# GpSimd writes the low half of a split weight tile in four pieces instead of one operation

## The chip, the core and the metric

The kernel runs on one core of a Trainium2 chip. Its time is the device time of one execution in microseconds (us), given as the median of several runs. The core's engines run their own instruction queues side by side and wait for one another by semaphores: TensorE (PE in the profile, with PEld for its weight loads), VectorE (DVE), ScalarE (ACT), GpSimd (POOL) and SyncE (SP, which issues most transfers).

## The reference, cut to what matters

One inference step of a two-layer model on 128 context tokens and 512 latent tokens (640 in all) of width 1024. Layer 0 mixes by a gated linear attention beside a latent attention, layer 1 by differential attention; each layer ends in a gated MLP.

```
for l in range(2):
    h  = modulate(rmsnorm(x, norm_gain[l, 0]), shift, scale)
    # layer 0: gated linear attention and latent attention, then one output projection
    # layer 1: q, k, v = split(h @ w_in_odd); rotary positions on q and k of the latent tokens
    #          per head: p = softmax(q1 k1) - lam * softmax(q2 k2); o = p @ v
    x  = x + gate * mixer(h)
    h  = modulate(rmsnorm(x, norm_gain[l, 1]), ...)
    u  = conv3(h @ w_up);  a, g = split(u)
    x  = x + gate * ((silu(a) * g) @ w_down)
y = rmsnorm(x, final_gain)
```

All of it is float32. The kernel gets close to that with three matmuls of a shorter type: every operand is written as a high half and a low half, and hi·hi + hi·lo + lo·hi is summed.

## The kernel before, in words

Activations lie with the 1024 features on the partitions (8 tiles of 128) and the 640 tokens along the free axis; `A` and `B` each hold such an array as a pair (high half, low half). Weights come from memory as tiles `wraw` of 128 partitions x 1024 numbers, seen as [128, 8, 128] (8 blocks `k` of 128 columns) or [128, 4, 256]. `Weights.split` (lines 161 to 166) makes the pair: ScalarE copies `wraw` into `whi` (line 163), and the engine that `eng` names subtracts `whi` from `wraw` into `wlo` (line 165). That engine is VectorE in most places and GpSimd in 33: in 5 tiles of the first projection (`ada0`, shape [128, 2, 512]), in 3 tiles of the MLP's `up` of each layer (line 959), and, from `W.eng = G` (line 1138) on, in 22 tiles in the stretch of layer 1's differential attention (19 of its projections, 3 of the output projection that follows).

In that attention the heads come in pairs. While the heads of one pair are worked on, `diff_units` makes the queries, keys and values of the next pair as filling between the steps: `unit_qk` (line 1062) multiplies a weight tile with `B` in two halves of 320 tokens (`proj_half`, matmuls `qko` at line 211), and rotates the result with `rope` (lines 475 to 481). In `rope` VectorE shuffles (`rsh`, line 478) and multiplies (line 479), GpSimd multiplies `f` by `ropeC` (line 480), and VectorE adds the two (line 481); `split` (lines 172 and 173) then makes the pairs `kd` and `qd`. A step of the attention itself (`Attn`) is: scores (PE, `sc`, line 826), minimum (DVE, `mn`, line 851) and exponential (ACT, `p`, line 852); the two maps are combined into `p` (ACT line 1098, then DVE line 1099, which reads two arrays of 128 x 768 from SBUF); PE transposes `p` (`ptp`, line 869), ACT and DVE write the pair `pt` from PSUM (lines 177 and 178), and PE multiplies by the values (`pv`, line 883).

```
S.copy(out=hi, in_=raw)
lo = self.tile("lo", shape, FP32R)
(eng or self.eng).tensor_tensor(out=lo, in0=raw, in1=hi.bitcast(FP32), op=ALU.subtract)
```

The order of the instructions on each engine is set when the program is built: a scheduler goes through the operations in the order of the code, with a timing model of its own, and places each on its engine's queue. Waits are set by regions: an instruction waits for those that wrote what it reads.

Of the kernel before, what the change touches and what calls it, by code (L numbers as in the profile page):

```python
# [7 lines left out]
FP32 = mybir.dt.float32  # L8
# [6 lines left out]
ALU = mybir.AluOpType  # L15
# [41 lines left out]
def build(tc, a):  # L57
    nc = tc.nc
    V, S, G, PE = nc.vector, nc.scalar, nc.gpsimd, nc.tensor
# [77 lines left out]
    class Weights:  # L137
# [23 lines left out]
        def split(self, raw, shape, eng=None):  # L161
            hi = self.tile("hi", shape, FP32R)
            S.copy(out=hi, in_=raw)  # L163
            lo = self.tile("lo", shape, FP32R)
            (eng or self.eng).tensor_tensor(out=lo, in0=raw, in1=hi.bitcast(FP32), op=ALU.subtract)  # L165
            return hi, lo

        def close(self):
# [129 lines left out]
    def apply_norm(tp, x, bc, hl, l, n, half, k0=0, k1=KT):  # L298
        c0, c1 = CH[half]
        for k in range(k0, k1):  # L300
            t = tp.tile([128, CUT], FP32, tag="nm_t", name="nm_t", bufs=3)[:, 0:c1 - c0]
            hi, lo = [z[:, k, c0:c1] for z in hl]
            for s0, s1, c in seg(c0, c1):
                r = slice(s0 - c0, s1 - c0)
                u, sh = t[:, r], mods[l][:, 3 * n * KT + k, c:c + 1]
                V.scalar_tensor_tensor(out=u, in0=x[:, k, s0:s1], scalar=gs[l][:, n, k, c:c + 1], in1=bc[:, r],  # L306
                                       op0=ALU.mult, op1=ALU.mult)
                S.activation(out=u if k % 2 else hi[:, r], in_=u, func=ACTF.Identity, bias=sh)
                if k % 2 == 0:
                    last = V.scalar_tensor_tensor(out=lo[:, r], in0=u, scalar=sh, in1=hi[:, r].bitcast(FP32),  # L310
                                                  op0=ALU.add, op1=ALU.subtract)
            if k % 2:
                split(t, hi, lo, G)
        return last
# [83 lines left out]
    V.memset(csil, 0.0)  # L398
    tables(S.activation(out=csil[:, :, 0:2], in_=sm["cT"], func=ACTF.Silu))
    split(csil[:, :, 0:2], csr[:, :, 0:2], csr[:, :, 2:4])  # L400

    awp, awes = pool("aw", side="left")
# [110 lines left out]
    def logsig(c):  # L513
        e = ab[:, c].rearrange("p (d n) -> p d n", d=2)
        V.scalar_tensor_tensor(out=e, in0=zmm(c), scalar=0.0, in1=e, op0=ALU.min, op1=ALU.subtract)
        split(ab[:, c].rearrange("p (g t) -> p g t", g=4), *[z[:, :, c * 128:(c + 1) * 128] for z in la])
# [35 lines left out]
    for q in range(4):  # L552
        w = W(a["wva"][q], [128, 2, 512])
        for kk in range(2):
            k = 2 * q + kk
# [799 lines left out]
```

## Time and profile before

| what | value |
|---|---|
| median of 3 runs | 1824.09 us (1821.87 to 1824.63) |
| the profiled execution | 1819.55 us, its span 1817.8 us |
| PE busy | 1744.3 us, 96% of the span |
| DVE busy | 1272.0 us, 70% |
| ACT busy | 758.9 us, 42% |
| POOL busy | 294.7 us, 16% |

The span is the part of the execution between the first and the last instruction; the rest of the profiled execution's time lies around it. The durations below come from this one execution. Times in rows are microseconds from the start of the span unless a column says ns.

### The profile page before, as it was taken

Reading aid. Unit: us, or ns where it says so; the run is one execution under the profiler, and the core shown is the slowest. Engines: PE = TensorE matmul, PEld = TensorE weight load, DVE = VectorE, ACT = ScalarE, POOL = GpSimd, SP = SyncE. Lnnn points to the kernel's source line nnn. Section 1 sums busy time; section 2 is a strip of 40 time slices with the busy share of each in tenths; the row PEclk is TensorE's granted clock in tenths of the full one; section 3 lists DMA queues with packets and bytes.
Section 4 is the critical chain, followed back from the end, with each engine's and each line's share of the span. In section 5 each row is a group of like instructions: output and inputs, shape, how many; then the busy total and the mean of one; then the engine's idle time right before and its main releaser. Section 6 shows DMA issues by size and latency. Waiting matters only on the chain. (4 is left out here: it accounts for less than half of the span.)

```text
span 1817.8 us, 29362 instructions
## 1 busy us (share of the span) xinstructions
PE 1744.3 (96%) x11716; PEld 1634.6 (90%) x11716; DVE 1272.0 (70%) x2438; ACT 758.9 (42%) x1344; POOL 294.7 (16%) x246
## 2 busy tenths in 40 slices
PE   7999989999999999999999999999999999999996
PEld 1898776889999999999988989897989999999996
DVE  5964877778699999946588787876475554545556
ACT  6444434544532232323356665665373232322232
POOL 3201021000310100100133232321031010101004
PEclk9999999999999999999999989998999999999998
DMA  9650001044256555412231021111122222222121
GB/s 372 198 166 9 28 3 72 4 175 139 93 174 189 171 176 184 156 59 88 65 123 61 31 58 42 63 49 70 59 70 81 82 70 79 73 73 79 59 82 58
DMA packets 57336, 176.58 MB, mean 97 GB/s; under 512 B 6064, under 2 KB 11568, under 8 KB 56816
## 3 DMA queue, kind: packets, MB, share of 16 engines
q1 hardware_dynamic: 53408, 160.59, 27.4%
q0 software_dynamic: 3792, 14.13, 2.2%
q8 instruction: 92, 1.51, 0.3%
q14 instruction: 44, 0.36, 0.1%
HBM read 166.59 MB, written 7.77 MB: 96 GB/s over the span
## 5 line engine op out<-in xcount | busy, mean ns | idle before, releaser
L202 PE MATMUL up<-B,whi 128*128 128x320 f32 x2560 | 479.6, 309 | 0.0
L163 ACT CAST whi<-wraw 128x1024 fp32r<-128x1024 f32 (+2 forms) x208 | 208.3, 1002 | 506.7 <-PE up L202 231.3
L202 PEld LDWEIGHTS up<-B,whi 128*128 128x128 f32 x2560 | 401.6, 188 | 0.0
L165 DVE TENSOR_TENSOR wlo<-wraw,whi 128x1024 fp32r<-128x1024 f32 (+2 forms) x175 | 204.2, 1167 | 226.3 <-ACT whi L163 226.0
L202 PE MATMUL up<-B,wlo 128*128 128x320 f32 x1280 | 291.8, 309 | 0.0
L202 PE MATMUL po<-A,whi 128*128 128x320 f32 x1312 | 246.3, 310 | 0.7 <-DVE u L967 0.5
L202 PEld LDWEIGHTS up<-B,wlo 128*128 128x128 f32 x1280 | 213.8, 188 | 0.0
L363 DVE CUSTOM_DVE_ANT_0 junk<-araw,cbc 128x1024 bf16<-128x1024 f32 x160 | 203.5, 1272 | 12.2 <-DMA araw<-in_wada0b 9.4
L202 PEld LDWEIGHTS po<-A,whi 128*128 128x128 f32 x1312 | 205.7, 188 | 1.5 <-issue 0.7
L173 POOL TENSOR_TENSOR A<-u,A 128x640 fp32r<-128x640 f32 x44 | 76.1, 1730 | 758.2 <-ACT A L172 733.2
L202 PE MATMUL po<-A,wlo 128*128 128x320 f32 x656 | 149.8, 310 | 0.5 <-DVE wlo L165 0.5
L211 PE MATMUL qko<-B,whi 128*128 128x320 f32 x512 | 121.6, 322 | 2.4 <-ACT B L172 1.5
L340 PE MATMUL pot<-A,whi 128*128 128x320 f32 x512 | 113.9, 312 | 0.0
L202 PEld LDWEIGHTS po<-A,wlo 128*128 128x128 f32 x656 | 109.5, 188 | 0.8 <-DVE wlo L165 0.8
L165 POOL TENSOR_TENSOR wlo<-wraw,whi 128x1024 fp32r<-128x1024 f32 x33 | 79.1, 2400 | 146.9 <-ACT whi L163 146.5
L965 DVE SCALAR_TENSOR_TENSOR u<-up,small,u 128x127 f32<-128x127 f32 (+1 forms) x176 | 95.5, 543 | 10.4 <-ACT u L963 9.5
L967 DVE SCALAR_TENSOR_TENSOR u<-up,small,u 128x127 f32<-128x127 f32 (+1 forms) x176 | 96.3, 548 | 4.5
L852 ACT ACTIVATE p<-sc,mn 128x768 f32<-128x768 f32 (+1 forms) x100 | 79.2, 797 | 39.8 <-DVE mn L851 39.3
L211 PEld LDWEIGHTS qko<-B,whi 128*128 128x128 f32 x512 | 89.0, 196 | 5.2 <-ACT B L172 1.8
L851 DVE TENSOR_REDUCE mn<-sc 128x1 f32<-128x768 f32 (+1 forms) x100 | 79.3, 816 | 16.1 <-PE sc L826 15.3
L340 PEld LDWEIGHTS pot<-A,whi 128*128 128x128 f32 x512 | 85.7, 188 | 1.1 <-issue 0.4
L202 PE MATMUL pe<-B,whi 128*128 128x320 f32 x416 | 81.2, 317 | 4.3 <-DVE nm_t L306 3.6
(294 smaller groups left out, 3056.0 us busy)
## 6 DMA issues: line engine op xcount, KB each, us to landing
wraw<-in_wup SPq DMA_DIRECT2D x88, 512.0 KB, 3.6
araw<-in_wada SPq DMA_DIRECT2D x48, 512.0 KB, 3.4
wraw<-in_wdn SPq DMA_DIRECT2D x40, 512.0 KB, 3.6
araw<-in_wada0b SPq DMA_DIRECT2D x32, 512.0 KB, 4.3
wraw<-in_wie SPq DMA_DIRECT2D x13, 512.0 KB, 4.4
aw<-in_wada0a SPq DMA_DIRECT2D x8, 512.0 KB, 8.8
wraw<-in_wada0a SPq DMA_DIRECT2D x8, 512.0 KB, 8.0
wraw<-in_woe SPq DMA_DIRECT2D x8, 512.0 KB, 4.3
```

The costliest lines, as they stand in the source:

```text
L163: S.copy(out=hi, in_=raw)
L165: (eng or self.eng).tensor_tensor(out=lo, in0=raw, in1=hi.bitcast(FP32), op=ALU.subtract)
L173: return (lo_eng or V).tensor_tensor(out=lo, in0=src, in1=hi.bitcast(FP32), op=ALU.subtract)
L202: PE.matmul(out=o, lhsT=w[wi][:, k], rhs=hl[ri][:, k, c0:c1], start=k == 0 and n == 0, stop=k == nk - 1 and n == 2)
L211: PE.matmul(out=o, lhsT=w[wi][:, k], rhs=hl[ri][:, k, c0:c1], start=k == 0 and n == 0, stop=k == nk - 1 and n == 2)
L340: PE.matmul(out=o, lhsT=ws[j + m][wi][:, k], rhs=hl[ri][:, k, c0:c1], start=k == 0 and n == 0, stop=k == nk - 1 and n == 2)
L363: V.tensor_tensor_reduce(out=junk, in0=raw, in1=self.cbc[:, j], op0=ALU.mult, op1=ALU.add, scale=1.0, scalar=0.0, accum_out=mods[l][:, t0 ...
L851: V.tensor_reduce(out=mn[:, m:m + 1], in_=ss[m][:, 0:nk], op=ALU.min, axis=AX.X)
L852: self.exp = S.activation(out=p[:, m, 0:nk], in_=ss[m][:, 0:nk], func=ACTF.Exp, scale=-1.0, bias=mn[:, m:m + 1], accum_out=li[:, m:m + 1])
L965: V.scalar_tensor_tensor(out=u[:, s0 + 1:s1], in0=r[:, s0:s1 - 1], scalar=cw[:, 0:1], in1=u[:, s0 + 1:s1], op0=ALU.mult, op1=ALU.add)
L967: last = V.scalar_tensor_tensor(out=u[:, s0:s1 - 1], in0=r[:, s0 + 1:s1], scalar=cw[:, 2:3], in1=u[:, s0:s1 - 1], op0=ALU.mult, op1=ALU.add)
```

## The change

The subtraction on GpSimd is cut along the second axis of the tile when that axis divides by four: a tile [128, 8, 128] or [128, 4, 256] becomes four operations of 128 x 256. The tiles [128, 2, 512] of the first projection stay whole, and so does every tile that VectorE subtracts. 28 operations become 112.

```
             lo = self.tile("lo", shape, FP32R)
-            (eng or self.eng).tensor_tensor(out=lo, in0=raw, in1=hi.bitcast(FP32), op=ALU.subtract)
+            eng = eng or self.eng
+            n = shape[1]
+            step = n // 4 if eng is G and n % 4 == 0 else n
+            for k in range(0, n, step):
+                z = slice(k, k + step)
+                eng.tensor_tensor(out=lo[:, z], in0=raw[:, z], in1=hi[:, z].bitcast(FP32), op=ALU.subtract)
             return hi, lo
```

Five lines are added, so that line numbers after 165 are five higher in the changed kernel. Each `qko` group of matmuls, which waited once for its tile's `wlo`, now waits four times, ahead of the first matmul on each piece. SyncE's queue is the same. The scheduler's order moves a little on the other engines, all of it in the differential attention.

GpSimd's queue in the second pair of heads, before. The first row fetches cached keys; the second is the weight tile of a query projection (`wlo`); then the rotary multiplications of the second head's queries and of the next pair's keys.

```order
L1072 DMA fk<-in_dkc 128x256
L165 TENSOR_TENSOR wlo<-wraw,whi 128x1024
L480 TENSOR_TENSOR fq<-fq,ropeC 128x192
L165 TENSOR_TENSOR wlo<-wraw,whi 128x1024
L480 TENSOR_TENSOR fq<-fq,ropeC 128x320
L1078 DMA o_dk<-fk 128x128
L480 TENSOR_TENSOR fk<-fk,ropeC 128x192
L165 TENSOR_TENSOR wlo<-wraw,whi 128x1024
L480 TENSOR_TENSOR fk<-fk,ropeC 128x320
L1072 DMA fk<-in_dkc 128x256
```

The same stretch with the change:

```order
L1077 DMA fk<-in_dkc 128x256
L170 TENSOR_TENSOR wlo<-wraw,whi 128x256 x4
L485 TENSOR_TENSOR fq<-fq,ropeC 128x192
L170 TENSOR_TENSOR wlo<-wraw,whi 128x256 x4
L485 TENSOR_TENSOR fq<-fq,ropeC 128x320
L1083 DMA o_dk<-fk 128x128
L485 TENSOR_TENSOR fk<-fk,ropeC 128x192
L170 TENSOR_TENSOR wlo<-wraw,whi 128x256 x4
L485 TENSOR_TENSOR fk<-fk,ropeC 128x320
L485 TENSOR_TENSOR fq<-fq,ropeC 128x192
```

Each `wlo` is now four operations in the place of one, and the rotary multiplication behind it stays behind all four. At the end the fetch of cached keys and the multiplication of 192 query tokens have changed places.

VectorE's queue about 40 us later, in the step that makes the next pair's first keys and queries, before. `li` and `p` belong to the attention, `fk`, `fq`, `rsh`, `kd` and `qd` to the rotation, `vd`, `vf` and `pt` are written from PSUM:

```order
L481 TENSOR_TENSOR fk<-fk,rsh 128x320
L1097 TENSOR_SCALAR li<-li,scal 128x1
L1099 SCALAR_TENSOR_TENSOR p<-p,li 128x768
L173 TENSOR_TENSOR kd_10866<-fk,kd_10865 128x320
L478 STREAM_SHUFFLE rsh<-fq 128x192
L479 TENSOR_TENSOR rsh<-rsh,ropeS 128x192
L178 TENSOR_TENSOR vd_11067<-vo,vd_11066 128x256
L1050 COPY vf<-vo 128x256
L178 TENSOR_TENSOR pt_10974<-ptp,pt_10973 128x3x128
L481 TENSOR_TENSOR fq<-fq,rsh 128x192
L178 TENSOR_TENSOR pt_10974<-ptp,pt_10973 128x3x128
L173 TENSOR_TENSOR qd_11020<-fq,qd_11019 128x320
```

With the change:

```order
L1102 TENSOR_SCALAR li<-li,scal 128x1
L486 TENSOR_TENSOR fk<-fk,rsh 128x320
L1104 SCALAR_TENSOR_TENSOR p<-p,li 128x768
L483 STREAM_SHUFFLE rsh<-fq 128x192
L178 TENSOR_TENSOR kd_10899<-fk,kd_10898 128x320
L484 TENSOR_TENSOR rsh<-rsh,ropeS 128x192
L486 TENSOR_TENSOR fq<-fq,rsh 128x192
L183 TENSOR_TENSOR vd_11109<-vo,vd_11108 128x256
L1055 COPY vf<-vo 128x256
L178 TENSOR_TENSOR qd_11056<-fq,qd_11055 128x320
L183 TENSOR_TENSOR pt_11007<-ptp,pt_11006 128x3x128 x2
```

The two additions of the rotation (`fk<-fk,rsh`, `fq<-fq,rsh`) and the low halves behind them have moved by one to three places: the first addition to behind a small operation on `li`, the second, with `qd`, to ahead of the two writes of `pt`.

## Rows read from the trace of the kernel before

**Rows 1.** The page's head, and its part on the engines: busy time, share of the span, instructions.

```profile
span 1817.8 us, 29362 instructions
PE 1744.3 (96%) x11716; PEld 1634.6 (90%) x11716; DVE 1272.0 (70%) x2438; ACT 758.9 (42%) x1344; POOL 294.7 (16%) x246
```

**Rows 2.** The waits of PE over the whole span: who waited for whom, us in total, times, longest.

```profile
PE pv L883 <- DVE pt L178: 6.9, 6, 2.0
...
PE adaps L424 <- POOL wlo L165: 2.4, 2, 1.6
```

**Rows 3.** All instructions of line 165 (count, ns min/median/max, first and last start), and below it who waited for that line (us, times); of these the rows of PEld and those for tiles that VectorE subtracts are left out.

```profile
L165 POOL TENSOR_TENSOR wlo<-wraw,whi x33: 2344/2394/2822, 7.9 to 1361.5; 128x1024 fp32r<-128x1024 f32 x33
...
who waited for it (us, times):
...
  PE adaps L424: 2.4, 2
```

**Rows 4.** The timeline about 1053 us, by engine (DVE, then POOL, ACT, PE): start, duration, engine, line, output and inputs, count; in brackets the idle time before it and what ended it.

```profile
1053.02 3.48 DVE L1099 SCALAR_TENSOR_TENSOR p<-p,li 128x768 f32<-128x768 f32 x1 [0.93 <-ACT p L1098]
...
1056.70 1.00 DVE L178 TENSOR_TENSOR pt<-ptp,pt 128x384 fp32r<-128x384 f32 x2
...
1053.32 2.36 POOL L165 TENSOR_TENSOR wlo<-wraw,whi 128x1024 fp32r<-128x1024 f32 x1
...
1053.20 0.87 ACT L177 CAST pt<-ptp 128x384 fp32r<-128x384 f32 x2
...
1054.55 0.74 PE L261 MATMUL rb<-negs,racc 128*64 128x2 f32 x10
1057.30 1.62 PE L883 MATMUL pv<-pt,vd 128*128 128x256 f32 x9 [2.00 <-DVE pt L178]
```

**Rows 5.** The same place one pair of heads later: DVE, POOL, PE.

```profile
1138.47 3.48 DVE L1099 SCALAR_TENSOR_TENSOR p<-p,li 128x768 f32<-128x768 f32 x1 [0.93 <-ACT p L1098]
...
1138.76 2.36 POOL L165 TENSOR_TENSOR wlo<-wraw,whi 128x1024 fp32r<-128x1024 f32 x1
...
1142.74 1.71 PE L883 MATMUL pv<-pt,vd 128*128 128x256 f32 x9 [2.01 <-DVE pt L178]
```

**Rows 6.** And in the last pair.

```profile
1220.88 2.39 DVE L1099 SCALAR_TENSOR_TENSOR p<-p,li 128x768 f32<-128x768 f32 x1 [0.93 <-ACT p L1098]
...
1220.09 2.37 POOL L165 TENSOR_TENSOR wlo<-wraw,whi 128x1024 fp32r<-128x1024 f32 x1 [2.21 <-ACT whi L163]
...
1224.07 1.33 PE L883 MATMUL pv<-pt,vd 128*128 128x256 f32 x9 [0.92 <-DVE pt L178]
```

**Rows 7.** All instructions of line 1099: ns min/median/max.

```profile
L1099 DVE SCALAR_TENSOR_TENSOR p<-p,li x40: 334/1018/3481, 963.8 to 1263.8; 128x768 f32<-128x768 f32 x32, 128x128 f32<-128x128 f32 x8
```

**Rows 8.** Two places where GpSimd operations follow one another and VectorE wants two SBUF operands: the timeline about 984 us, POOL then DVE, and the final normalization, POOL then DVE.

```profile
984.06 2.37 POOL L165 TENSOR_TENSOR wlo<-wraw,whi 128x1024 fp32r<-128x1024 f32 x1 [4.49 <-ACT whi L163]
986.39 1.11 POOL L480 TENSOR_TENSOR fq<-fq,ropeC 128x320 f32<-128x320 f32 x1
...
985.68 1.09 DVE L479 TENSOR_TENSOR rsh<-rsh,ropeS 128x320 f32<-128x320 f32 x1
...
1798.46 8.42 POOL L1183 TENSOR_TENSOR x2t<-x2t,bcs 128x320 f32<-128x320 f32 x8 [5.55 <-DVE bcs L245]
...
1803.34 2.82 DVE L234 TENSOR_TENSOR racc<-racc,rsq 128x320 f32<-128x320 f32 x3
```

**Rows 9.** The timeline of POOL at two operations of 128 x 256 that follow one another directly.

```profile
294.19 0.73 POOL L173 TENSOR_TENSOR A<-oo,A 128x256 fp32r<-128x256 f32 x1 [0.88 <-ACT A L172]
294.88 0.73 POOL L709 TENSOR_TENSOR oo<-oo,ga 128x256 f32<-128x256 f32 x1
```

**Rows 10.** Stretches of the span: us, then PE, PEld, DVE, ACT, POOL busy (instructions), the granted PE clock as a share of full speed, DMA share, GB/s.

```profile
1058.10:1061.50 3.40, 3.40 (x17) 3.40 (x16) 3.23 (x13) 2.63 (x6) 0.00 (x0) 0.50 0.18 74
...
1068.40:1075.10 6.70, 6.70 (x25) 5.63 (x24) 6.36 (x13) 3.67 (x8) 0.80 (x1) 0.50 0.29 81
...
1143.50:1146.80 3.30, 3.30 (x15) 3.30 (x15) 3.14 (x13) 2.48 (x6) 0.00 (x0) 0.50 0.17 71
1225.40:1228.70 3.30, 3.30 (x15) 3.30 (x15) 3.09 (x15) 3.05 (x6) 0.00 (x0) 0.50 0.04 11
...
1147.00:1218.00 71.00, 70.48 (x532) 64.76 (x531) 55.48 (x128) 43.52 (x98) 20.26 (x16) 1.00 0.11 36
```

**Rows 11.** The timeline of PE at three other waits.

```profile
985.77 1.30 PE L826 MATMUL sc<-kd,qd 64*128 64x512 f32 x6 [0.86 <-ACT p L852]
...
1067.41 1.51 PE L826 MATMUL sc<-kd,qd 64*128 64x512 f32 x6 [0.52 <-ACT p L852]
...
1152.85 1.31 PE L826 MATMUL sc<-kd,qd 64*128 64x512 f32 x6 [0.52 <-ACT p L852]
```

**Rows 12.** The rotary multiplication behind a weight tile and the addition that reads it, at two places: POOL and DVE about 1089 us, then about 1235 us.

```profile
1089.55 0.89 POOL L480 TENSOR_TENSOR fk<-fk,ropeC 128x320 f32<-128x320 f32 x1
...
1090.95 0.49 DVE L481 TENSOR_TENSOR fk<-fk,rsh 128x320 f32<-128x320 f32 x1
...
1234.77 1.20 POOL L480 TENSOR_TENSOR fq<-fq,ropeC 128x320 f32<-128x320 f32 x1
...
1236.55 0.48 DVE L481 TENSOR_TENSOR fq<-fq,rsh 128x320 f32<-128x320 f32 x1
```

## The prediction

> **What bounds the kernel now.** I read the page's busy shares first: PE is busy 96% of the span, 1744.3 of 1817.8 us, and POOL 16% [rows 1]. What can be won beside faster matmuls is therefore PE's 73.5 idle us and the time it runs at a lower clock. The obvious reading of the change is that PE can start on a piece of `wlo` before the whole tile is there. The waits say this is worth nothing: PE waited for a `wlo` of GpSimd in two places only, both in the first projection (`adaps`, 2.4 us), and those tiles are not cut [rows 2, 3].
>
> So I looked at what a GpSimd subtraction does to others. PE's longest sum of waits that is not a start-up is `pv`, waiting for VectorE's `pt`: 6.9 us [rows 2]. The timeline shows why. At 1053.02 VectorE starts line 1099, an operation on two SBUF arrays whose median is 1.018 us [rows 7]; it takes 3.48 us. GpSimd's `wlo` runs from 1053.32 to 1055.68, and line 1099 ends at 1056.50, 0.82 us after it [rows 4]. VectorE's operation stands still while GpSimd's runs. ScalarE has done its half of `pt` by 1054.07, but VectorE's half is queued behind line 1099 and starts at 1056.70; PE idles 2.00 us. The same rows return one pair later (3.48 us, PE idle 2.01) [rows 5] and in the last pair (2.39 us, idle 0.92) [rows 6]. Behind each of the three idle times PE runs 3.3 to 3.4 us at a granted clock of 0.50, the lower of its two levels, 1.2 instead of 2.4 GHz [rows 10].
>
> **The change part by part.**
>
> *A shorter hold.* What matters is whether VectorE gets its operands at the end of a piece, when the next piece is already queued. Two rows say yes. At 986.39 the rotary multiplication follows `wlo` directly on GpSimd, yet line 479, held since 985.68, ends at 986.77, while the multiplication takes 1.11 us instead of the 0.89 of another of its size [rows 8, 12]. And where eight GpSimd operations of 320 columns run back to back (8.42 us, 1.05 each), three of VectorE's end in 2.82 us, 0.94 each, about one GpSimd operation apart: they take turns [rows 8]. A piece costs 0.73 us, by a GpSimd subtraction of the same 128 x 256 [rows 9].
>
> First place: the first piece ends at 1053.32 + 0.73 = 1054.05, line 1099 at 1054.05 + 0.82 = 1054.87 instead of 1056.50, 1.63 us earlier; `pt` follows, and PE's 2.00 becomes 0.37. Second place: 1138.76 + 0.73 + 0.83 = 1140.32 against 1141.95, again 1.63, leaving 0.38. Third: `wlo` starts first, at 1220.09. Its second piece starts near 1220.8, about when line 1099 does (1220.88), so this waits to about 1221.55 and ends at 1222.36 instead of 1223.27, 0.91 earlier; PE's 0.92 goes. Sum 1.63 + 1.63 + 0.91 = 4.2 us. Behind these places PE has work and was not waiting, so I count it whole. VectorE's and GpSimd's rows there keep their order.
>
> Here a rule of the Trainium skill can be weighed (SBUF — State Buffer, "Who interferes with whom"): a VectorE operation with two SBUF inputs and a GpSimd operation that reads SBUF exclude each other, and the one that issues first keeps the port for its whole instruction. The trace agrees with the exclusion but not with the order: line 1099 started 0.30 us before GpSimd and still lost 2.46 us [rows 4]. By the rule it would win its race in the first two places, nothing would be left to gain there, and the sum would be the 0.91 of the third. The trace shows the loss, so I go by the rows.
>
> *The clock.* At half speed 3.4, 3.3 and 3.3 us of work cost 1.7 + 1.65 + 1.65 = 5.0 us [rows 10]. Do they go with the idle times? After a wait of 0.52 us the clock stayed at 1.00 at 1152.85 (the stretch 1147 to 1218), and after another of 0.52 at 1067.41 it was 0.50 for 6.7 us [rows 10, 11]. So for the 0.37 that is left both ends have a row: 0 and 5.0 us. I take half, 2.5.
>
> *GpSimd's own time.* Four pieces of 0.73, started 0.69 apart, end 3 x 0.69 + 0.73 = 2.80 us after the first start, against 2.39: 0.41 us for each of 28 tiles, 11.5 us on an engine that is 84% idle. In the MLP (six tiles) nothing waits. In the attention the rotary multiplication is behind the pieces, and VectorE's addition reads it. The room is small: it ended at 1090.44 and was read at 1090.95 (0.51 us), and at 1235.97, read at 1236.55 (0.58) [rows 12]. 0.41 fits. If VectorE's line 479 (0.34 after a release) is let in between the pieces, 0.75 does not. The scheduler has put one to three other operations ahead of these additions in most such places, which gives part of it back. Ends: 0, and eight places at 0.75 - 0.51 = 0.24, about 2 us. I take 0.6.
>
> *Waits and order.* Three more waits a tile on PE cost nothing if the pieces are there. At the first place `qko` follows `pv`, which ended at 1058.92 [rows 4] and would end near 1057.3; the last piece, with line 1099 let in, is done at 1053.32 + 2.80 + 0.82 = 1056.94. The moved rows on VectorE put `qd` and an addition, about 0.35 + 0.47 us, ahead of `pt` in two steps where PE had no wait; I count 0, and the danger is in the rivals.
>
> Sum: -4.2 - 2.5 + 0.6 = -6.1 us. On the profiled execution 1819.55 becomes 1813.45. The median of the runs lies 4.54 us above that execution (1824.09), and I carry the difference over: **1818.0 us**. The measurement tells about 0.2% (3.6 us) from no change, so this is just outside.
>
> **The rivals.**
>
> 1. *The clock stays low and VectorE gives some back*: 4.2 gained, 0 from the clock, 2 lost: -2.2, 1821.9 us, not measurable. For it: the 0.50 after a wait of 0.52 us [rows 10, 11]. Against: in the next pair the same wait had none.
>
> 2. *No release between pieces*: GpSimd keeps the operands while its queue holds the next piece. Then line 1099 is held 0.41 us longer in three places: +1.2, 1825.3 us, the same. Against it both cases of rows 8; for it, that there other lines, not pieces of one tile, followed each other.
>
> 3. *Slower: the additions of the rotation wait for GpSimd.* Every VectorE operation let in between pieces delays the rest by 0.34 to 0.82 us. With two or three of them the multiplication ends 0.41 + 1.5, about 1.9 us later, against 0.5 to 0.6 us of room [rows 12], and VectorE, with `pt` and `mn` queued behind the addition, stands 1.3 us. At eight places that is 10.4 us, less the 4.2, and with two new stretches at half clock (3.4) +9.6: 1833.7 us. It decides from about 0.6 us a place on, where eight places outweigh the gain. Against: in rows 4 to 6 and 8 one such operation falls into each `wlo`, not three.
>
> 4. *More than forecast*: all 5.0 us of clock, the 6.7 us stretch at 1068.4 (3.35 us [rows 10]), which follows a wait in the same pair, and the 0.86 at 985.77, which falls into another `wlo` [rows 8, 11]: -4.2 - 5.0 - 3.35 - 0.86 = -13.4, 1810.7 us.
>
> **How the numbers follow.** The forecast 0.48 (1814.9 with all three stretches gone to 1819.9 with none), rival 1 0.17, rival 2 0.10, rival 3 0.12, rival 4 0.13. Faster by over 0.2% are the forecast and rival 4: 0.61. The same: 0.27. Slower: 0.12. The range reaches from rival 4 to rival 2, 1811 to 1826 us; outside it stay rival 3 and the far side of rival 4.
>
> **What would show it.** Right: GpSimd's line 170 with 117 instructions, pieces of about 0.73 us; line 1104 with a longest duration near 1.9 us instead of 3.48; the wait of `pv` for `pt` at about 3 us instead of 6.9; fewer stretches at 0.50 in the pairs; the `wlo` waits of PE still in `adaps` alone. Wrong: line 1104 still at 3 us or more (rival 2), waits of VectorE for GpSimd's line 485 (rival 3), or the waits gone but the same number of stretches at 0.50 (rival 1).

## The result, and the profile after

The changed kernel takes 1808.63 us (median of 4 runs, 1807.67 to 1814.41), the kernel before, run beside it, 1822.98 (4 runs, 1821.79 to 1824.63): ratio 0.9935, 95% interval 0.9911 to 0.996, faster by more than the 0.2% that can be told. The forecast was 1818.0 in a range of 1811 to 1826. The sign is right; the gain is larger than the forecast, and the median lies 2.4 us under the lower end, nearest to the fourth rival (1810.7). By the ratio, the 1824.09 us that the forecast started from become 1812.2, just inside the range. The profiled execution took 1809.02 us for a span of 1807.2.

The page's head and engines, as [rows 1]:

```profile
span 1807.2 us, 29445 instructions
PE 1740.0 (96%) x11716; PEld 1628.6 (90%) x11716; DVE 1263.0 (70%) x2438; ACT 759.9 (42%) x1344; POOL 312.0 (17%) x330
```

POOL has 84 instructions more (28 tiles times 3) and is busy 17.3 us longer. The span is cut here at the same two points of the program, the first and the last long wait of PE in the differential attention; first the kernel before, then the changed one (us, then PE, PEld, DVE, ACT, POOL busy, the granted clock of PE, DMA share, GB/s):

```profile
0.00:961.00 961.00, 920.91 (x6055) 842.14 (x6056) 739.92 (x1405) 387.95 (x679) 135.81 (x122) 0.99 0.38 125
961.00:1286.00 325.00, 310.79 (x2211) 282.85 (x2210) 246.70 (x561) 194.14 (x428) 90.61 (x75) 0.94 0.16 52
1286.00:1817.00 531.00, 512.61 (x3452) 509.66 (x3452) 285.36 (x473) 176.86 (x239) 68.33 (x49) 0.98 0.24 74
```

```profile
0.00:963.00 963.00, 923.36 (x6056) 842.48 (x6056) 741.02 (x1405) 388.23 (x679) 136.99 (x131) 0.99 0.38 125
963.00:1275.00 312.00, 303.72 (x2211) 276.38 (x2209) 236.10 (x561) 194.55 (x428) 105.38 (x141) 0.97 0.17 54
1275.00:1807.00 532.00, 512.90 (x3452) 509.69 (x3452) 285.86 (x473) 177.11 (x240) 69.60 (x58) 0.98 0.24 74
```

All of the gain is in the middle, 325 to 312 us for the same 2211 matmuls. PE's idle time there goes from 14.2 to 8.3 us (5.9 less) and its busy time from 310.8 to 303.7 (7.1 less), at a granted clock of 0.97 of full speed instead of 0.94. These are two single executions; how much of the clock goes with the change is taken up below. The first part is 2 us longer and the last 1.

The waits of PE, as [rows 2], the line of VectorE's operation, as [rows 7], and GpSimd's subtractions:

```profile
PE adaps L429 <- POOL wlo L170: 3.4, 2, 1.8
...
PE pv L888 <- DVE pt L183: 1.2, 3, 0.5
```

```profile
L1104 DVE SCALAR_TENSOR_TENSOR p<-p,li x40: 335/1018/1495, 965.4 to 1253.7; 128x768 f32<-128x768 f32 x32, 128x128 f32<-128x128 f32 x8
```

```profile
L170 POOL TENSOR_TENSOR wlo<-wraw,whi x117: 717/742/2466, 8.8 to 1353.3; 128x256 fp32r<-128x256 f32 x112, 128x1024 fp32r<-128x1024 f32 x5
```

PE's waits for a GpSimd tile are still in the first projection alone, so no wait shows that a piece ready early could have shortened. The wait of `pv` for `pt` is 1.2 us in all instead of 6.9. Line 1104 (1099 before) has 1.50 us at its longest, not 3.48. At the first place, as [rows 4] (timeline of DVE, POOL, PE):

```profile
1054.83 1.47 DVE L1104 SCALAR_TENSOR_TENSOR p<-p,li 128x768 f32<-128x768 f32 x1 [0.65 <-ACT p L1103]
...
1056.50 1.00 DVE L183 TENSOR_TENSOR pt<-ptp,pt 128x384 fp32r<-128x384 f32 x2
```

```profile
1054.83 0.56 POOL L1077 DMA_DIRECT2D fk<-in_dkc  x1
1055.41 3.68 POOL L170 TENSOR_TENSOR wlo<-wraw,whi 128x256 fp32r<-128x256 f32 x4
```

```profile
1056.89 0.74 PE L266 MATMUL rb<-negs,racc 128*64 128x2 f32 x10
1057.56 1.79 PE L888 MATMUL pv<-pt,vd 128*128 128x256 f32 x9
```

`pt` ends at 1057.50 and PE goes on at 1057.56 with no wait where it stood 2.00 us. But look at the durations: VectorE's 1.47 us end 0.89 us after the first piece began, and the four pieces take 3.68 us, not the 2.80 that the prediction worked out. VectorE, which began as the issue of the `fk` load began (1054.83), ended 0.91 us after this issue did; it did not wait for a piece, the first piece waited for it. The second place is the same (1.50 us). In the last pair, as [rows 6]:

```profile
1213.25 1.45 DVE L1104 SCALAR_TENSOR_TENSOR p<-p,li 128x768 f32<-128x768 f32 x1 [0.76 <-ACT p L1103]
```

```profile
1212.46 3.53 POOL L170 TENSOR_TENSOR wlo<-wraw,whi 128x256 fp32r<-128x256 f32 x4 [0.66 <-PE ptp L874]
```

Here the operation began behind a piece, was held to its end, and took 1.45 us, against 1.48 by the prediction.

### The profile page after: what moved, and what is told of

Same layout as the page of the kernel before. It is cut to its first block, busy times and chain, and to the rows that moved or that the text cites. A ratio compares the mean times of both kernels' runs of the same rounds, so it can differ in the third digit from the quotient of the medians.

```text
span 1807.2 us, 29445 instructions
## 1 busy us (share of the span) xinstructions
PE 1740.0 (96%) x11716; PEld 1628.6 (90%) x11716; DVE 1263.0 (70%) x2438; ACT 759.9 (42%) x1344; POOL 312.0 (17%) x330
## 3 DMA queue, kind: packets, MB, share of 16 engines
q8 instruction: 92, 1.51, 0.3%
## 5 line engine op out<-in xcount | busy, mean ns | idle before, releaser
L170 POOL TENSOR_TENSOR wlo<-wraw,whi 128x256 fp32r<-128x256 f32 (+1 forms) x117 | 97.8, 865 | 134.5 <-ACT whi L163 133.8
L856 DVE TENSOR_REDUCE mn<-sc 128x1 f32<-128x768 f32 (+1 forms) x100 | 79.2, 815 | 14.6 <-PE sc L831 14.2
```

What stands on the lines that cost most here:

```text
L170: eng.tensor_tensor(out=lo[:, z], in0=raw[:, z], in1=hi[:, z].bitcast(FP32), op=ALU.subtract)
L856: V.tensor_reduce(out=mn[:, m:m + 1], in_=ss[m][:, 0:nk], op=ALU.min, axis=AX.X)
```

## The experiments

Three theories were put against each other. A: the gain is the shorter hold of VectorE's line 1104. B: it is the new order of rows that the scheduler gives the attention when the program has other instructions. C: PE starts earlier on a piece. Later D to G, told in the expectations, ask why a piece holds VectorE less. Ratios are to the kernel before, run on the same chip beside the experiment; they compare all runs and are not the quotient of two medians. The line numbers of these kernels lie 0 to 4 above those of the changed one, so VectorE's line is 1104, 1106 or 1108.

### Which tiles carry the gain

First I took the tile that collides at the first two places for that of `q1`, the query weights of the second head of a pair.

```diff
-            step = n // 4 if eng is G and n % 4 == 0 else n
+            step = n // 4 if eng is G and self.q1 else n      # a1; a2: n % 4 == 0 and not self.q1
...
+                W.q1 = isq and h % 2 == 1
                 w = W(a["wqo" if isq else "wko"][h], [128, KT, 128])
+                W.q1 = False
```

> The tiles of the unit q1 (the query weights of the second head of a pair, four tiles) are subtracted in four pieces; the other 24 that the change splits go in one operation. The order of the rows is then that of the kernel before but for 4 rows of VectorE and 3 of PE. Theory A (the gain is VectorE's line 1104 held for one piece instead of a whole tile at the three places of the prediction, with the low clock behind them): nearly all of the change's gain is there, 1808 to 1815 us, ratio about 0.994; line 1104 at most near 1.9 us instead of 3.48; the idle times of 2.00, 2.01 and 0.92 us fall to 0.4 or less. Theory B (the gain is the moved order of the rows in the attention): no gain, 1819 to 1824 us, whatever line 1104 takes. Theory C (PE starts earlier on a piece of any tile): four of 28 tiles, a seventh of the gain, 1821 us.

> The counterpart: the 24 other tiles in four pieces, the tiles of q1 in one operation. The order of ScalarE's rows is that of the changed kernel, and so is that of PE and VectorE but for 3 and 4 rows. Theory A: line 1104 is held as before (3.4 to 3.5 us at its longest), PE's two idle times of about 2 us and the low clock behind them are back, 1819 to 1825 us, ratio 0.998 to 1.002. Theory B: all the gain, 1808 to 1811 us, ratio 0.9935. Theory C: six sevenths of the gain, 1811 us.

Splitting `q1` alone gives 1820.17 us, ratio 1.0001 (0.9987 to 1.0015); all the others but `q1` give 1811.88, 0.9964 (0.9947 to 0.9981). Taken as written this speaks for B. The timelines say that the premise was wrong: with `q1` alone split, the tile at the place is whole, and all is as before:

```profile
1055.15 2.36 POOL L170 TENSOR_TENSOR wlo<-wraw,whi 128x1024 fp32r<-128x1024 f32 x1
```

```profile
1054.51 3.81 DVE L1106 SCALAR_TENSOR_TENSOR p<-p,li 128x768 f32<-128x768 f32 x1 [0.59 <-ACT p L1105]
```

```profile
1059.12 1.92 PE L888 MATMUL pv<-pt,vd 128*128 128x256 f32 x9 [2.26 <-DVE pt L183]
```

It stands behind the loads of `vc` and `fk` on GpSimd, and is that of `q0` of the next pair. So the pair was run again with `q0` (three tiles are GpSimd's). These two kernels are a cleaner test than the first: with `q0` alone split every row of PE, VectorE and ScalarE stands in the order of before, with all but `q0` split in that of the changed kernel.

```diff
-            step = n // 4 if eng is G and n % 4 == 0 else n
+            step = n // 4 if eng is G and self.qz else n      # c1; c2: n % 4 == 0 and not self.qz
...
+                W.qz = isq and h % 2 == 0
                 w = W(a["wqo" if isq else "wko"][h], [128, KT, 128])
+                W.qz = False
```

> The tile that lies on VectorE's line 1104 at the first two places is that of q0, the query weights of the first head of the next pair (its rows on GpSimd stand behind the loads of vc and fk), not that of q1. Here only these three tiles are split, the rest of the kernel is that of before, with every row of PE, VectorE and ScalarE in the order of before. Theory A (shorter hold): line 1104's counterpart falls from 3.5 to about 2 us at its longest among the first two places, PE's 2.00 and 2.01 us fall to about 0.4 each, the 0.92 us in the last pair stays: 3.3 us, and up to 6.8 us with the low clock behind them; ratio 0.994 to 0.998. Theory B (moved order): ratio 1.000, within 0.0015, although the idle times shrink or not. Theory C (early start of PE on a piece): three of 28 tiles, ratio 0.999 or more.

> The counterpart: the changed kernel, but the three tiles of q0 in one operation each; every row of PE, VectorE and ScalarE stands in the order of the changed kernel. Theory A: line 1104 takes 3.4 to 3.5 us at two places again, PE's idle times there are back (1.5 to 2.0 us, twice), ratio to the kernel before 0.998 to 1.001. Theory B: all of the gain, ratio 0.993 to 0.995, and the two idle times do not matter. Theory C: nine tenths of the gain, 0.994.

Three tiles in four pieces: 1811.16 us, ratio 0.9956 (0.9937 to 0.9975). The other 25 in pieces and these three whole: 1823.88 us, 1.0005 (0.9987 to 1.0024). A holds; B falls (the changed order alone gains nothing that can be measured), and C falls too. The rows of the first, at the first place:

```profile
1057.76 1.18 DVE L1106 SCALAR_TENSOR_TENSOR p<-p,li 128x768 f32<-128x768 f32 x1 [0.94 <-ACT p L1105]
```

```profile
1057.48 0.56 POOL L1079 DMA_DIRECT2D fk<-in_dkc  x1
1058.06 3.66 POOL L170 TENSOR_TENSOR wlo<-wraw,whi 128x256 fp32r<-128x256 f32 x4
```

```profile
1059.96 1.65 PE L888 MATMUL pv<-pt,vd 128*128 128x256 f32 x9
```

The rows of the second, with the order of the changed kernel:

```profile
1055.33 3.65 DVE L1106 SCALAR_TENSOR_TENSOR p<-p,li 128x768 f32<-128x768 f32 x1 [0.77 <-ACT p L1105]
```

```profile
1055.22 0.56 POOL L1079 DMA_DIRECT2D fk<-in_dkc  x1
1055.80 2.37 POOL L170 TENSOR_TENSOR wlo<-wraw,whi 128x1024 fp32r<-128x1024 f32 x1
```

```profile
1059.78 1.33 PE L888 MATMUL pv<-pt,vd 128*128 128x256 f32 x9 [1.77 <-DVE pt L183]
```

The order is worth something small: PE's wait is 1.77 us instead of 2.00, because PE comes to `pv` a little later there. The third place is the output projection's tile; with it and `q0` split, and nothing else:

```diff
+            W.qz = True
             self.pt, self.w, self.k, self.after = pt, W(wo, [128, 8, 128]), 0, after
+            W.qz = False
```

> The three tiles of q0 and the three tiles of the output projection (woo, in the last pair) split, the other 22 whole; the order of the rows is that of before but for 2 rows of VectorE. Theory A: all three places are relieved, 4.2 us and the clock behind them, ratio 0.993 to 0.996, as good as the changed kernel with 18 instructions more on GpSimd instead of 84. Theory B: ratio 1.000.

1810.22 us, ratio 0.9943 (0.9923 to 0.9964), the changed kernel's within the intervals. Six of 28 tiles carry what can be measured, and the other 22 cost nothing that can be measured.

### Where PE begins

```diff
-            for k in range(0, n, step):
+            for k in reversed(range(0, n, step)):
```

> The changed kernel with the pieces of each tile written from the last to the first, so that PE, which reads them from the first to the last, finds its first piece done only with the whole tile. Theory A: as the changed kernel, 1807 to 1812 us, line 1104 at most near 1.6 us. Theory C: the gain is lost, 1820 us or more, and PE shows waits for the tiles on GpSimd.

1809.18 us, 0.9939 (0.9921 to 0.9956): the last piece first changes nothing, so C falls here too. The scheduler ordered this kernel anew (115 of VectorE's 2438 places hold another operation than in the changed one), and the time is the same, which speaks against B once more.

### Without GpSimd

```diff
-                w = W(a["wqo" if isq else "wko"][h], [128, KT, 128])
+                w = W(a["wqo" if isq else "wko"][h], [128, KT, 128], V if isq and h % 2 else None)
```

(on the kernel before, so no tile is split)

> The kernel before with the four tiles of q1 subtracted by VectorE instead of GpSimd, in one operation (1.17 us each by the other tiles that VectorE subtracts), nothing split. No GpSimd operation falls on line 1104 at the three places. Theory A: line 1104 at most near 1.5 us, the three idle times of PE go unless VectorE's 1.17 us takes their place: 1810 to 1818 us. Theory C: nothing gained, 1822 us or more, since VectorE has 1.17 us more to do in four places.

1825.34 us, ratio 1.0033 (1.002 to 1.0046), slower. The premise on `q1` was wrong here as well, but the shift in time took the `q0` tile off line 1104 all the same (1.67 us at its longest). The next whole tile then fell on two other operations of VectorE:

```profile
1070.46 3.04 DVE L283 TENSOR_TENSOR rdg<-nid,ry 64x320 f32<-64x320 f32 x2
```

```profile
1070.46 2.69 POOL L170 TENSOR_TENSOR wlo<-wraw,whi 128x1024 fp32r<-128x1024 f32 x1 [4.59 <-ACT whi L163]
```

```profile
1073.64 0.77 PE L287 MATMUL rbc<-rdg,negs 64*128 64x320 f32 x2 [1.78 <-DVE rdg L283]
```

### How long a piece

```diff
-            step = n // 4 if eng is G and n % 4 == 0 else n
+            step = n // 2 if eng is G and n % 2 == 0 else n
```

> The changed kernel with two pieces of 128 x 512 instead of four. A piece is then about half of 2.36 us, and line 1104, which starts 0.3 us ahead of it, is held to its end: about 1.2 + 0.8 + 0.3 = 2.3 us at the longest instead of 1.9 or 3.48. Theory A: PE's two idle times are 0.3 to 1.0 us, the time lies between the changed kernel and the one before, ratio 0.995 to 0.998. Theory B: the rows are scheduled anew here too, so that any ratio from 0.99 to 1.01 could come out, without regard to line 1104.

1815.6 us, 0.9961 (0.9943 to 0.9979), in the range given, but not by the working given: line 1104 takes 3.64 us, more than beside a whole tile, and PE's two waits are 1.51 us.

```profile
L1104 DVE SCALAR_TENSOR_TENSOR p<-p,li x40: 335/1019/3643, 963.5 to 1253.6; 128x768 f32<-128x768 f32 x32, 128x128 f32<-128x128 f32 x8
```

A half does not let VectorE in at its end at these two places, though the last pair's operation was let in between two halves (1.31 us). The waits that shrank, twice 0.5 us and the 0.92 of the last pair, are 1.9 us, less than the gain; what gives the rest is not shown. As this kernel's rows are also ordered anew, the halves were given to `q0` alone, and beside that 256 and 768 columns:

```diff
-            step = n // 4 if eng is G and n % 4 == 0 else n
-            for k in range(0, n, step):
-                z = slice(k, k + step)
+            step = n // 4 if eng is G and self.qz else n      # d1; d2: n // 2, and the loop as it was
+            for k in (0, step)[:1 + (step < n)]:
+                z = slice(k, n if k else step)
```

> The three tiles of q0 in two unequal pieces, 128 x 256 and then 128 x 768; all else and every row of PE, VectorE and ScalarE as before. In the earlier traces VectorE's operation, begun 0.29 us ahead, went on at its own pace (1.18 us) while a first piece of 256 columns took twice its time (1.47 instead of 0.73), and lost everything to a first piece of 512 (3.64 us). Theory D (the length of the first piece decides who stands still): the operation takes 1.2 us, the piece 1.5, PE's two idle times are gone, the time is that of the three tiles in four pieces, ratio 0.994 to 0.997. Theory E (it is the release at the end of each piece, so the length of all pieces counts): the operation is let in behind the first piece, 1.9 us, or loses to the 768 columns as well, 3.5 us or more; ratio 0.997 to 1.001.

> The three tiles of q0 in two halves of 128 x 512, all else and every row of PE, VectorE and ScalarE as before. Theory D: the first half is long enough to stop VectorE, and the second follows without letting it in: 3.6 us for the operation, PE's idle times 2.1 to 2.3 us, ratio 0.999 to 1.002. Theory E: the operation ends 0.8 us behind the first half, 2.4 us, idle times of 0.9 us, ratio 0.996 to 0.999.

Halves: 1821.03 us, 0.9999 (0.9983 to 1.0015). The operation takes 3.62 us:

```profile
1052.99 3.62 DVE L1106 SCALAR_TENSOR_TENSOR p<-p,li 128x768 f32<-128x768 f32 x1 [0.93 <-ACT p L1105]
```

```profile
1052.71 0.56 POOL L1079 DMA_DIRECT2D fk<-in_dkc  x1
1053.29 2.50 POOL L170 TENSOR_TENSOR wlo<-wraw,whi 128x512 fp32r<-128x512 f32 x2
```

So D holds for the durations. 256 and 768 columns: 1825.05 us, 1.0019 (1.0003 to 1.0036), and the time that D gives is wrong, although the durations are right: the operation takes 1.18 us and PE's two waits at `pv` are gone. The new loss is some 9 us later, and the same again in the next pair, so that 5.9 us of new idle time stand against the 4.0 that are gone:

```profile
1055.54 1.18 DVE L1106 SCALAR_TENSOR_TENSOR p<-p,li 128x768 f32<-128x768 f32 x1 [0.93 <-ACT p L1105]
...
1064.65 2.31 DVE L277 SCALAR_TENSOR_TENSOR ry<-rt,ry 64x10 f32<-64x10 f32 x1
```

```profile
1067.62 1.31 PE L287 MATMUL rbc<-rdg,negs 64*128 64x320 f32 x4 [2.95 <-DVE rdg L283]
```

GpSimd's next tile, whole in this kernel, runs from 1064.59 to 1066.93, and an operation of ten columns that takes 0.16 us elsewhere begins 0.06 us behind it and stands 2.31 us. The relief at one place moved VectorE into the next long hold. With `q0` alone in four pieces that tile came later (1068.32) and met nothing that PE waited for. The changed kernel splits that tile too, so that no whole tile stands there.

### Who stands still

Two runs measured it on arrays of their own, behind the end of the program, with a GpSimd subtraction and a copy of VectorE's operation (1.02 us alone), started by ScalarE at chosen distances. One pair, written out:

```diff
+                S.copy(out=p0[:, 0:1], in_=go[:, 0:1])
+                S.copy(out=scr[:, 0:m], in_=p0[:, 0:m])
+                S.copy(out=gi[:, 0:1], in_=scr[:, 0:1])
+                V.scalar_tensor_tensor(out=vo[:, 0:768], in0=p0[:, 0:768], scalar=ml[:, 0:1], in1=p1[:, 0:768], op0=ALU.mult, op1=ALU.add)
+                G.tensor_tensor(out=go[:, 0:n], in0=gi[:, 0:n], in1=gj[:, 0:n], op=ALU.subtract)
```

> The changed kernel with 30 pairs of operations behind its end, on arrays of their own: a GpSimd subtraction of 128, 256, 384, 512 or 1024 columns and a VectorE operation of 128 x 768 with two SBUF inputs (1.02 us alone), VectorE's begun from about 0.2 us behind to about 1 us ahead of GpSimd's. Theory D: up to 256 columns the GpSimd operation waits for VectorE's, which takes 1.0 to 1.2 us, wherever VectorE began first; from 512 columns on VectorE's stands still until GpSimd's ends, and takes up to 3.5 us beside 1024 columns, even if it began first. The rule that whoever begins first keeps the port: the size does not matter, VectorE's takes 1.0 to 1.2 us in every pair in which it began first. The time of the whole kernel is longer by the pairs, some 100 us, and says nothing.

D falls as a general rule. In all 30 pairs VectorE began first, by 0.10 to 1.09 us (none came out with GpSimd first), in 25 of them it was still at work when GpSimd's operation began, and it always took its 1.02 us, whatever the size; GpSimd's operation waited (1024 columns: 2.61 us instead of 2.34 when it began 0.61 us behind).

```profile
L1217 DVE SCALAR_TENSOR_TENSOR mvo<-mp,ml,mp x30: 1017/1018/1020, 1812.0 to 1878.4; 128x768 f32<-128x768 f32 x30
```

```profile
1868.59 2.61 POOL L1214 TENSOR_TENSOR mgo<-mgi,mgj 128x1024 f32<-128x1024 f32 x1 [0.86 <-ACT mgi L1229]
```

What the two places of the kernel have and these pairs do not is a load that GpSimd issues when VectorE begins. The last run put one or two such loads ahead of the subtraction (the first line of the cut stands in 16 of the 28 pairs).

```diff
+                nc.gpsimd.dma_start(out=dv2, in_=a["dvc"][:, :, 0:256])
+                nc.gpsimd.dma_start(out=dt2, in_=a["dkc"][:, 0])
+                for k0, k1 in zip(cuts, cuts[1:]):
+                    G.tensor_tensor(out=go[:, k0:k1], in0=gk[:, k0:k1], in1=gj[:, k0:k1].bitcast(FP32), op=ALU.subtract)
```

> The changed kernel with eight pieces of 128 x 128 instead of four, and behind its end 28 more pairs, on arrays of their own: GpSimd issues one load or two (those of fk and vc, 0.56 and 0.76 us in the traces) and then subtracts 1024 columns whole, in two halves, in four quarters, or in 256 + 768, while VectorE's operation of 128 x 768 with two SBUF inputs begins during the loads' issue or soon after. In the pairs without a load (the run before this) whoever began first kept the port, at every size. Theory F (the issue of a load on GpSimd is what makes the difference: VectorE is held from the issue on): VectorE takes 3.4 to 3.7 us beside the whole tile and beside two halves, 1.2 to 1.5 us beside four quarters and beside 256 + 768, as at the two places of the kernel, whenever it begins during the issue. Theory G (the load's issue has no part in it): VectorE, begun first, takes 1.0 to 1.2 us in all of them. The main part with eight pieces: the first two places show an operation of 1.2 to 1.5 us and no idle time of PE over 0.5 us there, GpSimd is busier by some 15 us than with four pieces, and PE does not wait for it.

F holds in its first half: VectorE's operation loses although it began before the subtraction, if it began while GpSimd issued the `fk` load, or late in the issue of the `vc` load ahead of it. It then stands not to the end of one GpSimd instruction but of all that are queued, beside two halves as beside a whole tile. With both loads ahead, as in the kernel, four quarters let it in when the issue ends. Two halves, then twice four quarters:

```profile
1911.20 0.55 POOL L1238 DMA_DIRECT2D mdt<-in_dkc  x1
1911.77 2.49 POOL L1240 TENSOR_TENSOR mgo<-mgk,mgj 128x512 fp32r<-128x512 f32 x2
...
1927.11 0.55 POOL L1238 DMA_DIRECT2D mdt<-in_dkc  x1
1927.68 3.47 POOL L1240 TENSOR_TENSOR mgo<-mgk,mgj 128x256 fp32r<-128x256 f32 x4
```

```profile
1911.29 3.79 DVE L1234 SCALAR_TENSOR_TENSOR mpp<-mpp,ml 128x768 f32<-128x768 f32 x1 [2.07 <-ACT mpp L1232]
...
1926.98 1.55 DVE L1234 SCALAR_TENSOR_TENSOR mpp<-mpp,ml 128x768 f32<-128x768 f32 x1 [4.23 <-ACT mpp L1232]
1932.93 1.32 DVE L1234 SCALAR_TENSOR_TENSOR mpp<-mpp,ml 128x768 f32<-128x768 f32 x1 [4.41 <-ACT mpp L1232]
```

Its second half does not hold everywhere: behind the `fk` load alone, neither quarters nor 256 and 768 columns let VectorE in:

```profile
1849.63 4.04 DVE L1234 SCALAR_TENSOR_TENSOR mpp<-mpp,ml 128x768 f32<-128x768 f32 x1 [3.71 <-ACT mpp L1232]
1855.17 3.81 DVE L1234 SCALAR_TENSOR_TENSOR mpp<-mpp,ml 128x768 f32<-128x768 f32 x1 [1.50 <-ACT mpp L1232]
```

Operations that began before any issue ran their 1.02 us, and so did those that began 0.15 or 0.37 us into the `vc` load's issue with the `fk` load behind it, with every pattern. With both loads and 256 and 768 columns none was held, but only one began during the `fk` load's issue, 0.02 us into it, where the held ones had begun 0.08 or 0.09 us into it or 0.59 us into the `vc` load's, so this decides little; at the two places of the kernel with 256 and 768 columns VectorE began 0.28 us into the issue and was let in. The trace of before has a single load too: at 1008.11 line 1099 began while the `fk` load was issued, with a multiplication of 192 columns behind it, and took 1.66 us, until 0.83 us after that multiplication.

The main part of this kernel has eight pieces in the tiles of 128 x 8 x 128 and leaves the tiles of the value weights whole (their second dimension is 4). The first two places are relieved (1.21 us; the loads come later there, and the operation begins behind a piece), the subtractions take 110.0 us of GpSimd instead of 97.8, and the whole tile behind them does what it did with 256 and 768 columns: it falls on line 283, and PE stands 2.76 us, twice. The expectation looked at the first two places and did not foresee this wait.

```profile
1061.47 2.77 DVE L283 TENSOR_TENSOR rdg<-nid,ry 64x320 f32<-64x320 f32 x2
```

```profile
1061.15 2.34 POOL L170 TENSOR_TENSOR wlo<-wraw,whi 128x1024 fp32r<-128x1024 f32 x1 [3.45 <-ACT whi L163]
```

### Idle times and the clock

The granted clock differs from run to run of one kernel, and with it the time: over the 82 runs of the kernel before that stood beside these experiments it has a mean of 0.9795 of full speed at 1820.4 us, and 0.001 more goes with 1.27 us less (slope over the 82). By kernel, with the longest waits of PE at the first two places, or 7 to 15 us behind them, in the profiled execution:

| kernel | runs | mean us | mean granted clock | waits, us |
|---|---|---|---|---|
| before | 82 | 1820.4 | 0.9795 | 2.00, 2.01 |
| changed | 4 | 1809.8 | 0.9823 | 0.52, 0.52 |
| changed, last piece first | 6 | 1808.8 | 0.9828 | under 0.5 |
| `q0` split alone | 11 | 1812.8 | 0.9821 | 0.52, 0.52 |
| `q0` and output projection | 8 | 1810.6 | 0.9821 | 0.52, 0.52 |
| all but `q1` | 12 | 1813.1 | 0.9807 | 0.52, 0.42 |
| `q1` split alone | 12 | 1820.0 | 0.9806 | 2.26, 2.27 |
| all but `q0` | 12 | 1822.3 | 0.9763 | 1.77, 1.76 |
| all in halves | 12 | 1814.2 | 0.9801 | 1.51, 1.51 |
| `q0` in halves | 12 | 1820.8 | 0.9797 | 2.15, 2.15 |
| `q0` in 256 and 768 | 12 | 1824.6 | 0.9768 | 2.95, 2.95 |
| `q1` on VectorE | 12 | 1825.4 | 0.9759 | 1.78, 1.78 |

`q0` alone gains 7.6 us in the mean. Its clock is higher by 0.0026, which by the slope is 3.3 us; the other 4.3 are about the two idle times of 2.00 and 2.01. This is an estimate, as the slope is that of the runs of before. For `q0` with the output projection the same working gives 4.9 us of idle time and 3.4 by the clock, of 9.8 in all, so that 1.5 are left without an account; for all in halves it gives 1.9 and 0.8, of 6.2, and 3.5 are left. So the clock seems to give back somewhat less than the idle times themselves, and kernel by kernel it does not follow the waits: with waits of over 2 us left `q1` alone has 0.9806, and all but `q0`, with shorter waits than before, has 0.9763. Nor does it go place by place: the profiled execution with `q0` alone, at 1818.75 us against its median of 1811.16, is at the lower level for 3.4 us right behind the first relieved place and for 6.8 us behind each of the two waits of 0.52 us that follow.

## Why the prediction was right, and where it was off

**What bounds the kernel.** Right: the waits of `pv` for `pt` were what the change touches, and the early start of PE was worth nothing that can be measured.

**A shorter hold.** Right in place and sign, under-sized at 4.2 us, and half wrong in mechanism. In the last pair it is as worked out, held by one piece and let in at its end (1.45 against 1.48 us). At the first two places the step that lets line 1099 in at the end of the first piece, 1054.05, and ends it at 1054.87, failed. There VectorE began while GpSimd was still issuing the `fk` load, a row of the trace of before that the prediction did not read:

```profile
1052.74 0.56 POOL L1072 DMA_DIRECT2D fk<-in_dkc  x1
```

With a piece of 256 columns next it goes on when the issue ends, and the piece waits, so the gain is 2.30 us a place (3.48 to 1.18 with `q0` alone, in the order of before) and nothing is left of the 2.00 and 2.01, where 0.37 and 0.38 were forecast. For halves the same reasoning, theory E, left waits of 0.9 us a place; they are 2.15. It was luck that four pieces were the size to judge. The idle times taken away are 2.00 + 2.01 + 0.92 = 4.93 us. Another 1 us went from two waits further on (1.29 and 0.91 us before, 0.52 and 0.56 now), but with `q1` alone and with `q0` in halves these are 0.52 and 0.56 us as well, while the waits of the three places still stand; so they are not shown to come from the change.

**Who goes first.** The prediction set the trace against the Trainium skill (SBUF — State Buffer, "SBUF: two separate sides" and "Who interferes with whom"): a VectorE operation with two SBUF inputs and a GpSimd operation that reads SBUF exclude each other, and the one that starts first keeps the shared pair for the whole instruction. The prediction concluded that the order does not decide. Of plain operations this was wrong: in the 25 pairs that overlapped the first always kept it, as the Trainium skill says, and at every size. There the Trainium skill has it too: "Issue order, not op shape, decides who blocks". The two places are another case, a VectorE operation of two SBUF inputs that begins while GpSimd issues a load; there it stood 3.48 us although it began 0.30 us before the subtraction. The forecast went by the row and kept its sign thereby.

**The clock.** Mis-sized: 2.5 us taken, about 3.5 by the mean clock of the changed kernel and the slope above. In the profiled execution PE's busy time in the attention fell 7.1 us: two of the three stretches that were named are gone (1143.5 and 1225.4), the one of 6.7 us at 1068.4 that rival 4 took in, and 3.5 of 13.7 us in front of the output projection. The last two are not shown to come from the change: the profiled execution with `q1` alone, its waits of 2.26 and 2.27 us still there, runs the stretch behind 1069.6 at full clock too and has 10.2 us in front of the output projection. The reason for the half was the 0.37 us thought to be left. The stretch at 1058.1 is still there with no wait before it, however. The changed kernel at 1058.1, at 1068.4 and behind the second place, then `q1` alone:

```profile
1058.10:1061.50 3.40, 3.40 (x17) 3.40 (x16) 3.23 (x14) 2.80 (x6) 1.54 (x3) 0.52 0.40 111
1068.40:1075.10 6.70, 6.70 (x46) 6.07 (x45) 6.70 (x13) 4.35 (x10) 1.43 (x2) 1.00 0.31 81
1136.00:1143.00 7.00, 7.00 (x58) 6.72 (x58) 6.74 (x24) 3.79 (x8) 3.58 (x5) 1.00 0.42 150
```

```profile
1069.60:1076.40 6.80, 6.80 (x45) 6.13 (x44) 6.80 (x15) 4.18 (x9) 1.42 (x2) 1.00 0.24 80
```

**GpSimd's own time.** 0.6 us taken; one wait is all that shows, of VectorE for line 485:

```profile
  DVE fq L486: 0.3, 1
```

Rival 3 needed eight places. The pieces take longer than forecast (POOL 17.3 us more, 11.5 forecast); at the three places one of them waits for VectorE (1.45 to 1.49 us instead of 0.73), but no operation that PE needs stands behind them. **Waits and order** was right at 0: no new wait of PE.

Rival 2 (no release between pieces) was dismissed on handovers that are real, but it came true for halves, and for quarters behind a single load. Rival 4 named the size best, with 0.13, but not by all of its terms: the 0.86 us at 985.77 are still 0.84. Rival 1's low clock did not come as a whole, but it shows at the first place. What was mis-sized is the hold (4.2 us, measured 4.93) and the clock (2.5, about 3.5); together they make 8.4 of the 10.6 us between the means, and the rest stays open.

## What to carry to other kernels

A long GpSimd operation cost most here where a VectorE operation with two SBUF inputs stood behind it with PE waiting; look for a VectorE line whose maximum is several times its median, and read what GpSimd was doing when it began, loads that it issues included. Shorten all such operations of a stretch, not only the one that collides: relief at one place moved VectorE into the next whole tile in three kernels here, where PE then waited 1.78 to 2.95 us, and in the two of them whose time says something the gain was gone. An idle time of PE of 2 us can bring back more than itself by the clock behind it (7.6 us in the mean for 4.0 of idle time), but the clock scatters by as much from kernel to kernel, so this is a rough estimate.

## What the runs showed of the hardware that was not expected

- A VectorE operation on two SBUF arrays that begins while GpSimd issues a load can stand through everything queued on GpSimd: 3.48 us beside one operation of 1024 columns, 3.62 beside two of 512, 4.04 beside four of 256 behind a single load; alone it takes 1.02. Of ten columns, 0.16 us alone, it stood 2.31 us behind a subtraction that began 0.06 us earlier.
- Whether it is let in when the issue ends depended on the length of the next operation: with 256 columns and both loads ahead it was let in each time (1.18 to 1.50 us at the first two places of five kernels; in a sixth, where it began 0.01 us before the issue ended, behind the first piece, 1.60 and 1.61), with 512 or 1024 never (3.48 to 3.83 us at the first two places of five, before among them). Why a length should matter there, when it does not without a load, and why one load alone behaves otherwise than two, stays open.
